# GLA heads of a two-layer streaming encoder: eight places for the running states, the first rows of a head's output fetched early, and a norm's reciprocal root on VectorE

## The chip, the cores and the metric

The kernel runs on one core of a Trainium2 chip. The metric is the device time of one launch in microseconds, as the median of three runs. Traces come from the hardware profiler, of one execution each. TensorE (PE, with its weight loads PEld) multiplies; VectorE (DVE) and ScalarE (ACT) work on what it leaves in PSUM; GpSimd (POOL) and SyncE (SP) mostly issue DMAs, each in the order of its own queue.

## The reference

Two layers, each one pre-normed mixer with a residual, run over 512 frames of a new stream (prompt) and 16 frames of each of 8 running streams (sample), 640 tokens in all. Layer 0 is stick-breaking attention, layer 1 is gated linear attention (GLA) with 4 heads, key width 256 and value width 512. Layer 1 is the part at hand:

```python
b = jnp.cumsum(g, axis=1)
b_last = b[:, -1]
q_in = q * jnp.exp(b)
a = jnp.einsum('bchd,bshd->bhcs', q_in, k * jnp.exp(-b))
a = jnp.where(jnp.tril(jnp.ones((C, C), dtype=bool)), a, 0.0)
o = jnp.einsum('bhcs,bshe->bche', a, v) + jnp.einsum('bchd,bhde->bche', q_in, S)
S = jnp.exp(b_last)[..., None] * S + jnp.einsum('bshd,bshe->bhde', k * jnp.exp(b_last[:, None] - b), v)
...
o = o * lax.rsqrt(jnp.mean(o * o, axis=-1, keepdims=True) + EPS) * g_out.astype(f32).reshape(GLA_HEADS, GLA_DV)
y = (o.reshape(B, T, nv) * jax.nn.silu(r.astype(f32))).astype(h.dtype) @ w_out
```

For the running streams S starts from an input, `state_gla` (8 streams x 4 heads x 256 x 512 floats), and the updated states are an output. Everything is fp32.

## The kernel before, in words

An fp32 product is made of three products of halves in fp32r: every weight block and every row block is split by ScalarE (the high half, L134) and VectorE (the low half, L135, which needs the high one), and TensorE does high x high, low x high and high x low.

The program has one stage after the other; the one at hand is the stage of layer 1's heads. TensorE's order is written out by the program itself: a main line of products (`drive`) is interleaved with side lanes, generators that say by `step` how long they want to wait, counted in a planner's own estimate of TensorE's time. A step may also ask for PSUM banks, and a "tiled" step waits until a planner's interval between tiled groups has passed. This settles in which order instructions are issued; on the chip each engine takes its instructions in the order in which a scheduler has put them, and waits on semaphores. In this stage there are:

- **The main line.** First `others`, 24 parts of the input projection (L653): q and k of heads 1 to 3. Each part is stored to DRAM from a buffer `pl` (two of them). Then `share(0)` and `share(1)` (L699): the first eight of 16 row blocks of the output projection, four column blocks each, with five token blocks added into y. A share's weights come as raw pieces (`wraw`, SyncE's queue) that are then split. After the heads the rest of the output projection (L368), the last column block (L2004) and the final norm follow.
- **The decays** (`decays`): for each head the gates' running sum and its exponentials, applied to q and k (L1638 on TensorE, then ScalarE and VectorE up to k at L1664). Weights `wa2` have two buffers.
- **The prompt lane**: four chunks of 128 tokens for each head. Scores (L1566), masked by `copy_predicated` into one of three tiles `aT` that were zeroed once; products with values and state (L1554); the state's update on VectorE (S, L1757; S1l, L1692). The output is squared and summed by ScalarE (L1579), normed (`rstd_of`, below), scaled by ScalarE (L1583), turned by TensorE (L1601), multiplied with the gate (L1602) and stored as `og` to DRAM from GpSimd's queue.
- **The sample lane**: the 8 running streams. Their states are 64 blocks of 128 x 512 (head, half of the streams e, half of the key dimension dt, pair of streams m), taken in 16 groups of four. For a group TensorE multiplies q with the four states (L1864, eight instructions), then for each state the new k with v (L1870); VectorE updates the state in place (L1872), and GpSimd stores it (L78) and asks for the next state into a free place. There are S0 = 7 places in SBUF, so the n-th state is loaded into the place of state n-7 once that one's store has landed. State numbers in this text count from 0, so group n holds states 4n to 4n+3. The lane asks for its step 13 us of the planner's time after the last request of the group. A norm and an og store as in the prompt lane end a head.
- **The rows** (`fetches`): row blocks of og (128 x 640) come back from DRAM through the `pl` buffers (SyncE), are split into `ogh` and `ogl`, and are what a share multiplies with. For head 0 that begins when the last part has been issued; the first share is then planned once rows 0 to 3 are there.

`rstd_of` makes mean square plus epsilon on VectorE (L232) and takes its power -1/2 on GpSimd (L234), in the same queue as the loads and stores of states, gates and og:

```python
dve.tensor_scalar(ms, ss, 1.0 / n, EPS, op0=ALU.mult, op1=ALU.add)
nc.gpsimd.tensor_tensor(r, ms, mhalf[:, :w], op=ALU.pow)
```

Of the kernel before, what the change touches and what calls it, by code (L numbers as in the profile page):

```python
# [8 lines left out]
F32 = mybir.dt.float32  # L9
F32R = mybir.dt.float32r  # L10
U32 = mybir.dt.uint32
BF16 = mybir.dt.bfloat16
AF = mybir.ActivationFunctionType
ALU = mybir.AluOpType
# [16 lines left out]
ZSCALE = 128 ** -0.5  # L31
TOK = T // P
WR = 2
S0 = 7
GP = 2
NPAIR = HEADS // 2
PLAIN = 2
# [4 lines left out]
def hybrid_step_kernel(ctx: ExitStack, tc: tile.TileContext, A: dict, O: list):  # L42
# [185 lines left out]
    def rstd_of(pool, ss, n, name):  # L228

        w = ss.shape[1]  # L230
        ms = pool.tile([P, w], F32, tag=name + "_ms", name=name + "_ms")
        dve.tensor_scalar(ms, ss, 1.0 / n, EPS, op0=ALU.mult, op1=ALU.add)  # L232
        r = pool.tile([P, w], F32, tag=name + "_r", name=name + "_r")
        nc.gpsimd.tensor_tensor(r, ms, mhalf[:, :w], op=ALU.pow)  # L234
        return r

    def rstd_row(pool, ss, bc, a):

        turned_wide(wide_of(pool, rstd_of(pool, ss, D, "nrm")), bc, a)
# [37 lines left out]
    class Side:  # L277
# [10 lines left out]
        def after(self, wait, what):  # L288

            self.due.append((pe["now"] + wait, what))  # L290
            self.due.sort(key=lambda x: x[0])

        def share(self, **bufs):
            self.free = {k: [0.0] * n for k, n in bufs.items()}
# [387 lines left out]

    y_t = {}

    def share(g, og, w, leave=None, at=None, first=None):


        src = w.rearrange("(kt p) n -> p kt n", p=P)

        def raw(c, i):  # L690
            return wraw(src[:, 4 * g + 2 * i:4 * g + 2 * i + 2, 512 * c:512 * c + 512], 2, 512)

        def products(acc, a, i, w):
            wh, wl = w
            for e in range(2):
                kt = 4 * g + 2 * i + e
                h, lo = (x[:, P * a:P * a + P] for x in og[kt])
# [12 lines left out]
        raws = list(first or [raw(0, 0), raw(0, 1)])  # L710

        def made():
            return [t.rearrange("p (a n) -> p a n", a=2) for t in split(raws.pop(0))]

        w0, w1 = made(), made()
        for c in range(4):
            ws = [w0, w1]
            if c < 3:
                raws += [raw(c + 1, 0), raw(c + 1, 1)]
            if at:  # L720
                at(c)
            each = (0, 1, 2) if leave is add or c < 3 else (4, 1, 2, 3, 0)
            for a in each:
                acc = bank("mm")
                for i in range(2):
                    yield from products(acc, a, i, ws[i])
                leave(a, c, acc)
                if a == each[0] and c < 3:
                    w0 = made()
            if len(each) == 3:  # L730
                acc = {a: bank("mm") for a in (3, 4)}
                for i in range(2):
                    for a in (3, 4):
                        yield from products(acc[a], a, i, ws[i])
                        if i:
                            leave(a, c, acc[a])
                    if i == 0 and c < 3:
                        w1 = made()
# [762 lines left out]
        k0 = 4 * g + 2 * i  # L1501
        return w_out1.rearrange("(kt p) n -> p kt n", p=P)[:, k0:k0 + 2, 512 * c:512 * c + 512]

    with tc.tile_pool(name="gl", bufs=1, reuse_waits="tile") as gl:
        came = {"plain": False, "last": False, "of": 0, "when": 0.0}

        def keep(dst, hh):
            t = []

            def leave(nt, pt):  # L1510
# [11 lines left out]

        others = plain(h2, src, [(n0 + P * hh, keep(dst, hh)) for h in range(1, GH)
                                 for n0, dst in ((256 * h, gq_d[h]), (NK + 256 * h, gk_d[h])) for hh in range(2)],
                       lambda: came.update(plain=True))
        for _ in range(2):
            next(others)

# [24 lines left out]
            for n, (a, b) in enumerate(((0, 0), (0, 1), (1, 0))):  # L1553
                mm(out, l[a], by(l[a], r[b]), start=start and n == 0, stop=stop and n == 2, skip_group_check=True)  # L1554

        masked = [gl.tile([P, P], F32, name=f"aT{n}") for n in range(3)]
        for t in masked:
            nc.gpsimd.memset(t, 0.0)
        turns = {"n": 0}
# [15 lines left out]
        def normed(o):  # L1575

            s1 = gl.tile([P, 1], F32, tag="oss", name="oss", bufs=2)
            on = gl.tile([P, 512], F32, tag="on", name="on", bufs=2)
            act(on, o, AF.Square, accum_out=s1)  # L1579
            return on, rstd_of(gl, s1, 512, "on"), o  # L1580

        def scaled_by(on, r, o):
            act(on, o, AF.Copy, scale=r)  # L1583
# [25 lines left out]
        def decays():  # L1609

            def weights(h):
                wa2 = gl.tile([96, 256], F32R, tag="wa2", name="wa2", bufs=2)
                load(wa2.bitcast(F32), wa2_d[:, 256 * h:256 * h + 256])
                yield step(4.0 if h else 8.0)
                return wa2
# [183 lines left out]
        def sample_lane():  # L1799
# [12 lines left out]
            for h in range(GH):  # L1812
# [43 lines left out]
                for n in range(4):  # L1856
                    dt, e = n // 2, n % 2
                    group = [(h, e, dt, m) for m in range(4)]
                    while any(x not in states for x in group):
                        yield step(0.3)  # L1860
                    yield step(max(since, max(states[x][1] for x in group) + 13.0) - pe["now"], tiled=True)
                    for m in range(4):
                        l = qz[e][:, dt, 32 * m:32 * m + 32]
                        mm(o[32 * m:32 * m + 32, :], l, by(l, states[group[m]][0]), start=False, stop=n == 3,  # L1864
                           skip_group_check=True)
                    for m in range(4):
                        yield step(0.3, tp=1)
                        pt = bank("tp")
                        l = kst[e][:, m, :]
                        mm(pt, l, by(l, vst[:, m, :]), start=True, stop=True)  # L1870
                        s0 = states[group[m]][0]
                        dve.scalar_tensor_tensor(s0, s0, es[:, dt, 2 * m + e:2 * m + e + 1], pt,  # L1872
                                                 op0=ALU.mult, op1=ALU.add)
                        side.after(1.0, lambda x=group[m]: leaves(x))
                    if n == 1:
                        yield from stack(1)
                        yield step(1.5)
# [5 lines left out]
                if h + 1 < GH:  # L1883
                    yield step(4.0)
                    here = fetch(h + 1)

        def fetches():

            def free(kt):
                g, s = kt // 4, kt % 4  # L1890
                return came["plain"] and came["shares"] >= min(2, g if s > 1 else g - 1)

            rows = {}

            def ask_rows(kt):
                rows[kt] = gl.tile([P, T], F32, tag="pl", name="og_in", bufs=2)
                load(rows[kt], og_d[kt // 4][:, kt % 4, :])

            for kt in range(10):
                while min(through.values()) <= kt // 4 or not came["last"]:  # L1900
                    yield step(0.5)
                if kt not in rows:
                    yield step(5.0)
                    ask_rows(kt)
                    if kt % 4 < 3 and kt < 9 and came["plain"]:
                        ask_rows(kt + 1)
                    yield step(4.0)
                while not free(kt):
                    yield step(0.3)
                n = 20 + 2 * kt % 12  # L1910
                og1[kt] = slot(n, name="ogh"), slot(n + 1, name="ogl")
                halves(*og1[kt], rows.pop(kt))
                if kt % 4 < 3 and kt < 9 and kt + 1 not in rows:
                    ask_rows(kt + 1)
                came["rows"], came["at"] = kt + 1, pe["now"]
                yield step(0.5)
# [2 lines left out]
        for x in (decays(), prompt_lane(), sample_lane(), fetches()):  # L1919
            side.add(x)  # L1920
        drive(others)
        with tc.tile_pool(name="w4", bufs=1, reuse_waits="tile") as w4:
            ring3["pool"] = w4
            first = [wraw(w_of(0, 0, i), 2, 512) for i in range(2)]
            for g in range(2):
                side.until(lambda: came["rows"] >= 4 * g + 4 and pe["now"] > came["at"] + 2.0)
                drive(share(g, og1, w_out1, first=first))
                came["shares"] = g + 1
                first = [wraw(w_of(g + 1, 0, i), 2, 512) for i in range(2)]
            ring3["pool"] = None  # L1930
            parts = [split(r) for r in first]
            first = [wraw(w_of(3, 0, i), 2, 512) for i in range(2)]
            side.finish()


    share_banks(mm=8)
# [96 lines left out]
```

## Time and profile before

| | us |
|---|---|
| median of 3 runs (lowest, highest) | 2536.63 (2534.4, 2538.53) |
| the profiled execution | 2535.51 |
| its span | 2533.8 |
| stage of the heads | 1975.4 to 2413.0 |
| TensorE busy over the span | 2429.8 (96%) |
| VectorE, ScalarE, GpSimd busy | 1581.8, 995.2, 163.6 |
| mean granted clock of TensorE | 0.982 |

Rows of the profile read like this: start, duration, engine, line, operation, output<-input by the program's names, shapes, and in brackets the engine's idle time just before with what ended it. A row of waits is "who waits <- for whom: us in total, times, longest". A DMA row on POOL or SP shows its issue; it lands some microseconds later. Lines of the changed program are up to 22 higher than those of the program before (L78 becomes L79, L135 L136, L1864 becomes L1886, L1870 L1892, L699 L716, L653 L670, L1601 L1622).

### The profile page before, as it was taken

How to read it: one execution, taken by the hardware profiler on the slowest of the kernel's cores; microseconds unless marked ns; L12 is line 12 of the kernel's file. 1: busy time of each engine (PE TensorE's matmuls, PEld its weight loads, DVE VectorE, ACT ScalarE, POOL GpSimd, SP SyncE). 2: the span in 40 equal slices, each digit the busy share in tenths (PEclk: the TensorE clock that was granted, in tenths of full speed). 3: DMA queues.
4: the chain of work that ended last, by engine and by line, in shares of the span. 5: the costliest groups of instructions: out<-in, count | busy, mean ns of one | idle time of the engine just before them, and what ended most of it. 6: DMA issues, size and time to landing. Idle time of an engine off the chain costs nothing. (4 is left out here: it accounts for less than half of the span.)

```text
span 2533.8 us, 43960 instructions
## 1 busy us (share of the span) xinstructions
PE 2429.8 (96%) x17561; PEld 2150.1 (85%) x17561; DVE 1581.8 (62%) x2565; ACT 995.2 (39%) x1730; POOL 163.6 (6%) x390
## 2 busy tenths in 40 slices
PE   7899999999999989999999989999999999979998
PEld 5589999999999989888887768999999988857776
DVE  5575555555656655766775678666676565555556
ACT  4342222222223334555442345333333554545223
POOL 0010000000000000000000000000000233342100
PEclk8899999999999999999999999999999999989999
DMA  9966666766654357777864655354434778785634
GB/s 346 327 209 212 223 214 198 241 218 205 219 186 123 113 187 233 260 246 243 267 209 124 214 172 169 96 148 123 125 105 119 212 238 255 217 278 184 228 111 147
DMA packets 469439, 503.13 MB, mean 199 GB/s; under 512 B 42730, under 2 KB 366450, under 8 KB 469106
## 3 DMA queue, kind: packets, MB, share of 16 engines
q1 hardware_dynamic: 446274, 436.60, 54.8%
q0 software_dynamic: 16048, 51.92, 6.1%
q10 hardware_dynamic: 6912, 11.80, 1.3%
q8 instruction: 138, 2.26, 0.4%
q14 instruction: 67, 0.55, 0.1%
HBM read 411.10 MB, written 89.13 MB: 197 GB/s over the span
## 5 line engine op out<-in xcount | busy, mean ns | idle before, releaser
L594 PE MATMUL ps_mm<-sums,wh 128*128 128x320 f32 x2752 | 613.7, 311 | 1.5 <-ACT wh L134 1.5
L594 PE MATMUL ps_mm<-h,wh 128*128 128x320 f32 x2064 | 461.8, 312 | 5.7 <-DVE u L600 4.6
L594 PEld LDWEIGHTS ps_mm<-sums,wh 128*128 128x128 f32 x2752 | 458.3, 188 | 10.4 <-issue 7.4
L594 PE MATMUL ps_mm<-sums,wl 128*128 128x320 f32 x1376 | 425.8, 309 | 0.7 <-DVE wl L135 0.7
L135 DVE TENSOR_TENSOR wl<-wr,wh 128x1024 fp32r<-128x1024 f32 x193 | 236.1, 1224 | 244.0 <-ACT wh L134 243.2
L594 PEld LDWEIGHTS ps_mm<-h,wh 128*128 128x128 f32 x2064 | 343.2, 188 | 21.8 <-issue 13.0
L134 ACT CAST wh<-wb 128x1024 fp32r<-128x1024 f32 x170 | 178.4, 1049 | 426.1 <-PE ps_mm L594 352.8
L134 ACT CAST wh<-wr 128x1024 fp32r<-128x1024 f32 x193 | 202.6, 1050 | 346.6 <-PE ps_mm L594 184.6
L594 PE MATMUL ps_mm<-h,wl 128*128 128x320 f32 x1032 | 319.2, 309 | 0.0
L653 PE MATMUL ps_mm<-h,wh 128*128 128x320 f32 x1152 | 265.2, 318 | 5.3 <-ACT pl L1514 3.1
L594 PEld LDWEIGHTS ps_mm<-sums,wl 128*128 128x128 f32 x1376 | 258.4, 188 | 1.0 <-DVE wl L135 1.0
L135 DVE TENSOR_TENSOR wl<-wb,wh 128x1024 fp32r<-128x1024 f32 x170 | 207.9, 1223 | 60.5 <-ACT wh L134 60.1
L653 PEld LDWEIGHTS ps_mm<-h,wh 128*128 128x128 f32 x1152 | 193.0, 189 | 21.7 <-issue 11.4
L699 PE MATMUL ps_mm<-wh,ogh 128*128 128x512 f32 x450 | 197.4, 439 | 4.2 <-DVE y L704 2.7
L594 PEld LDWEIGHTS ps_mm<-h,wl 128*128 128x128 f32 x1032 | 193.8, 188 | 0.0
L653 PE MATMUL ps_mm<-h,wl 128*128 128x320 f32 x576 | 178.5, 310 | 0.0
L699 PE MATMUL ps_mm<-wh,ogl 128*128 128x512 f32 x450 | 177.9, 395 | 0.3 <-DVE ogl L135 0.3
L699 PE MATMUL ps_mm<-wl,ogh 128*128 128x512 f32 x450 | 177.7, 395 | 0.0
L699 PEld LDWEIGHTS ps_mm<-wh,ogh 128*128 128x128 f32 x450 | 85.6, 190 | 29.6 <-issue 14.4
L653 PEld LDWEIGHTS ps_mm<-h,wl 128*128 128x128 f32 x576 | 108.8, 189 | 0.0
L699 PEld LDWEIGHTS ps_mm<-wh,ogl 128*128 128x128 f32 x450 | 85.0, 189 | 20.3 <-DVE ogl L135 0.7
L518 PE MATMUL ps_mm<-wh,h 128*128 128x512 f32 x252 | 93.4, 432 | 5.9 <-ACT h L134 2.8
(355 smaller groups left out, 3747.0 us busy)
## 6 DMA issues: line engine op xcount, KB each, us to landing
ar<-in_w_ada_dram SPq DMA_DIRECT2D x160, 512.0 KB
wb<-in_sb_w_in_dram SPq DMA_DIRECT2D x82, 512.0 KB
kc<-in_cache_sb_k_dram SPq DMA_DIRECT2D x64, 512.0 KB
vc<-in_cache_sb_v_dram SPq DMA_DIRECT2D x64, 512.0 KB
wr<-in_gla_w_in_dram SPq DMA_DIRECT2D x51, 512.0 KB
wb<-in_gla_w_in_dram SPq DMA_DIRECT2D x45, 512.0 KB
wr<-in_sb_w_in_dram SPq DMA_DIRECT2D x44, 512.0 KB
ar<-in_w_ada_dram SPq DMA_DIRECT2D x64, 256.0 KB
```

Of the source, the lines that this page charges most:

```text
L134: nc.scalar.copy(hi, x)
L135: (e or dve).tensor_tensor(lo, x, hi.bitcast(F32), op=ALU.subtract)
L518: mm(acc[a], l, by(l, r[:, e, :]), start=j == 0 and e == 0 and begun, stop=j == 7 and e == 1 and last)
L594: mm(acc, l[:, k, :], by(l[:, k, :], r), start=start and k == 0 and first, stop=k == 7 and last, skip_group_check=True)
L653: mm(acc[nt], l[:, k, :], by(l[:, k, :], r), start=k0 == 8 and k == 0 and first, stop=k0 == 0 and k == 7 and last)
L699: mm(acc, l, by(l, r[:, e, :]), start=i == 0 and e == 0 and first, stop=i == 1 and e == 1 and last)
```

## The change

Four things are changed in the stage of the heads, and nothing ahead of it:

1. S0 is 8 instead of 7. The space for it comes from one `wa2` buffer less, and from two of the masked tiles, which are put into adaLN tables that are no longer read (`sh_t[1]`, `sc_t[1]`).
2. `rstd_dve` replaces `rstd_of` for the 20 norms of the heads: an integer guess of the reciprocal root, a cubic and a quadratic Newton step, nine VectorE instructions on 128x1, none on GpSimd. The norms of the layers and the final one keep `rstd_of`.
3. Rows 0 to 2 of head 0's output are loaded early into two tiles that the shares' split weights use later (row 2 in two pieces, so there is one load and one split more), and are split when the last but one part has ended. Row 3 and all later ones come through `pl` as before. The first share is begun inside the last part: its two first weight pieces are loaded and the first is split there.
4. The sample lane asks for an ordinary step at 9 us of the planner's time after the request, then for a tiled one, instead of a tiled one at 13 us. Some waits between looks are 0.3 instead of 0.5.

```diff
-S0 = 7
+S0 = 8
...
+    def rstd_dve(pool, ss, n, name):
+
+        ms, r, t, u = (pool.tile([P, 1], F32, tag=f"{name}_{x}", name=f"{name}_{x}", bufs=2 if x == "r" else 1) for x in ("ms", "r", "t", "u"))
+        dve.tensor_scalar(ms, ss, 1.0 / n, EPS, op0=ALU.mult, op1=ALU.add)
+        dve.tensor_scalar(r.bitcast(I32), ms.bitcast(I32), -0.5, float(0x5F3759DF), op0=ALU.mult, op1=ALU.add)
+        for cubic in (True, False):
+            dve.scalar_tensor_tensor(t, r, ms, r, op0=ALU.mult, op1=ALU.mult)
+            if cubic:
+                dve.tensor_scalar(u, t, 0.375, -1.25, op0=ALU.mult, op1=ALU.add)
+                dve.tensor_scalar(u, t, u, 1.875, op0=ALU.mult, op1=ALU.add)
+            else:
+                dve.tensor_scalar(u, t, -0.5, 1.5, op0=ALU.mult, op1=ALU.add)
+            dve.tensor_tensor(r, r, u, op=ALU.mult)
+        return r
...
-        w0, w1 = made(), made()
+        w0 = made()
+        if apart:
+            yield
+        w1 = made()
...
-                       lambda: came.update(plain=True))
+                       lambda: upper())
...
-        masked = [gl.tile([P, P], F32, name=f"aT{n}") for n in range(3)]
+        masked = [t[1].rearrange("p k r -> p (k r)")[:, :P] for t in (sh_t, sc_t)] + [gl.tile([P, P], F32, name="aT2")]
...
-            return on, rstd_of(gl, s1, 512, "on"), o
+            return on, rstd_dve(gl, s1, 512, "on"), o
...
-                wa2 = gl.tile([96, 256], F32R, tag="wa2", name="wa2", bufs=2)
+                wa2 = gl.tile([96, 256], F32R, tag="wa2", name="wa2")
...
-                    yield step(max(since, max(states[x][1] for x in group) + 13.0) - pe["now"], tiled=True)
+                    yield step(max(since, max(states[x][1] for x in group) + 9.0) - pe["now"])
+                    yield step(0.0, tiled=True)
...
+        def upper():
+            came.update(plain=True)
+            begun.append(share(0, og1, w_out1, first=[wraw(w_of(0, 0, i), 2, 512) for i in range(2)], apart=True))
+            next(begun[0])
...
+            x = [w4.tile([P, 1024], F32, tag=t, name="og_in") for t in ("wh", "wl")]
+            for n in range(2):
+                load(x[n][:, :T], og_d[0][:, n, :])
+            load(x[0][:, T:], og_d[0][:, 2, :1024 - T])
+            load(x[1][:, T:2 * T - 384], og_d[0][:, 2, 1024 - T:])
+            while not came["plain"]:
+                yield step(0.3)
+            for kt in range(2):
+                halves(*row(kt), x[kt][:, :T])
+                yield step(0.8)
+            to = row(2)
+            halves(*[t[:, :1024 - T] for t in to], x[0][:, T:])
+            halves(*[t[:, 1024 - T:] for t in to], x[1][:, T:2 * T - 384])
...
-            for kt in range(10):
+            for kt in range(3, 10):
...
-                drive(share(g, og1, w_out1, first=first))
+            drive(share(g, og1, w_out1, first=first) if g else begun[0])
```

GpSimd's queue around the load of state 47, the last of group 11, before. `s_23211` is state 40, whose place state 47 (`s_23486`) takes:

```order
L234 TENSOR_TENSOR on_r<-on_ms,mhalf 128x1
L78 DMA og_93<-gate 512x1x128
L78 DMA out_dram<-S 128x2x512
L78 DMA out_dram<-s_23211 128x512
L78 DMA out_dram<-s_23225 128x512
L78 DMA out_dram<-s_23227 128x512
L78 DMA gate<-gr_106 128x4x128
L78 DMA out_dram<-s_23339 128x512
L78 DMA og_93<-gate 512x1x128
L78 DMA s_23486<-in_state_gla_dram 128x512
```

The same with the change. State 47 is `s_23519`; it takes the place of state 39 (`s_22815`), and state 40 is `s_23329`:

```order
L79 DMA out_dram<-s_22773 128x512
L79 DMA out_dram<-s_22784 128x512
L79 DMA out_dram<-s_22803 128x512
L79 DMA s_23491<-in_state_gla_dram 128x512
L79 DMA out_dram<-s_22815 128x512
L79 DMA s_23493<-in_state_gla_dram 128x512
L79 DMA s_23511<-in_state_gla_dram 128x512
L79 DMA og_93<-gate 512x1x128
L79 DMA s_23519<-in_state_gla_dram 128x512
L79 DMA gate<-gr_105 128x4x128
L79 DMA og_93<-gate 512x1x128
L79 DMA out_dram<-s_23329 128x512
```

The load of state 47 has moved ahead of the store of state 40, the first of the group before it, and the root is gone from the queue.

TensorE's order at the end of the parts (`others`), before: the last two rows of L653, then the sample lane, a norm's transposes and head 3's decay, the states of group 11 (L1864), and the first share's products (L699):

```order
L653 MATMUL ps_mm<-h,wh 128x320 x2
L653 MATMUL ps_mm<-h,wl 128x320
L1870 MATMUL ps_tp<-vst,kst_20578 128x512 x3
L1601 MATMUL ps_tp<-ident,on 128x128 x4
L1638 MATMUL ps_tp<-alr_in,wa_22802 128x320 x2
L1864 MATMUL ps_z<-s_23356,qz_20577 32x512
L1864 MATMUL ps_z<-s_23378,qz_20577 32x512
L1864 MATMUL ps_z<-s_23402,qz_20577 32x512
L1864 MATMUL ps_z<-s_23486,qz_20577 32x512
L1870 MATMUL ps_tp<-vst,kst_20579 128x512
L699 MATMUL ps_mm<-wh,ogh 128x512
```

The same place with the change:

```order
L670 MATMUL ps_mm<-h,wh 128x320 x2
L670 MATMUL ps_mm<-h,wl 128x320
L1622 MATMUL ps_tp<-ident,on 128x128 x4
L1886 MATMUL ps_z<-s_23329,qz_20579 32x512
L1886 MATMUL ps_z<-s_23347,qz_20579 32x512
L1886 MATMUL ps_z<-s_23359,qz_20579 32x512
L1886 MATMUL ps_z<-s_23385,qz_20579 32x512
L1575 MATMUL ps_tp<-v,krh 128x512 x2
L1575 MATMUL ps_tp<-v,krl 128x512
L1892 MATMUL ps_tp<-vst,kst_20581 128x512 x4
L716 MATMUL ps_mm<-wh,ogh 128x512
```

The group at the border is now group 10 (states 40 to 43), not 11, whose products come inside the share.

VectorE's order at the same place, before: a norm's only VectorE step among the state updates and the splits of og rows:

```order
L135 TENSOR_TENSOR ogl<-og_in,ogh 128x640
L1838 TENSOR_TENSOR kc<-kd,kc 128x4x32
L1872 SCALAR_TENSOR_TENSOR s_23356<-s_23356,es,ps_tp 128x512
L232 TENSOR_SCALAR on_ms<-oss 128x1
L1872 SCALAR_TENSOR_TENSOR s_23378<-s_23378,es,ps_tp 128x512
L1872 SCALAR_TENSOR_TENSOR s_23402<-s_23402,es,ps_tp 128x512
L135 TENSOR_TENSOR ogl<-og_in,ogh 128x640
L1872 SCALAR_TENSOR_TENSOR s_23486<-s_23486,es,ps_tp 128x512
```

With the change, from the updates of group 10 to the end of that norm (the row in it is row 4; row 3 stands some rows ahead):

```order
L1894 SCALAR_TENSOR_TENSOR s_23329<-s_23329,es,ps_tp 128x512
L1894 SCALAR_TENSOR_TENSOR s_23347<-s_23347,es,ps_tp 128x512
L246 TENSOR_SCALAR on_u<-on_t 128x1
L1894 SCALAR_TENSOR_TENSOR s_23359<-s_23359,es,ps_tp 128x512
L1778 SCALAR_TENSOR_TENSOR S<-S,el,ps_tp 128x512
L1894 SCALAR_TENSOR_TENSOR s_23385<-s_23385,es,ps_tp 128x512
L247 TENSOR_SCALAR on_u<-on_t,on_u 128x1
L136 TENSOR_TENSOR ogl<-og_in,ogh 128x640
L250 TENSOR_TENSOR on_r<-on_r,on_u 128x1
L244 SCALAR_TENSOR_TENSOR on_t<-on_r,on_ms 128x1
L249 TENSOR_SCALAR on_u<-on_t 128x1
L250 TENSOR_TENSOR on_r<-on_r,on_u 128x1
```

The norm's steps now stand between the updates, and a row's split stands between its steps.

More of the change, by code (lines that the diff above doesn't have):

```diff
@@ L11 @@
 U32 = mybir.dt.uint32
+I32 = mybir.dt.int32
 BF16 = mybir.dt.bfloat16
@@ L290, in after @@
             self.due.append((pe["now"] + wait, what))
+            self.due.sort(key=lambda x: x[0])
             self.due.sort(key=lambda x: x[0])
@@ L683, in hybrid_step_kernel, with share @@
     y_t = {}
-    def share(g, og, w, leave=None, at=None, first=None):
+    def share(g, og, w, leave=None, at=None, first=None, apart=False):
         src = w.rearrange("(kt p) n -> p kt n", p=P)
@@ L1502, in w_of @@
         return w_out1.rearrange("(kt p) n -> p kt n", p=P)[:, k0:k0 + 2, 512 * c:512 * c + 512]
-    with tc.tile_pool(name="gl", bufs=1, reuse_waits="tile") as gl:
+    with tc.tile_pool(name="gl", bufs=1, reuse_waits="tile") as gl, \
+            tc.tile_pool(name="w4", bufs=1, reuse_waits="tile") as w4:
         came = {"plain": False, "last": False, "of": 0, "when": 0.0}
@@ L1885, in sample_lane, with row @@
                     here = fetch(h + 1)
+        begun = []
+        def upper():
+            came.update(plain=True)
+            begun.append(share(0, og1, w_out1, first=[wraw(w_of(0, 0, i), 2, 512) for i in range(2)], apart=True))
+            next(begun[0])
+        def row(kt):
+            n = 20 + 2 * kt % 12
+            og1[kt] = slot(n, name="ogh"), slot(n + 1, name="ogl")
+            return og1[kt]
         def fetches():
@@ L1890, in free @@
                 g, s = kt // 4, kt % 4
-                return came["plain"] and came["shares"] >= min(2, g if s > 1 else g - 1)
+                return came["shares"] >= min(2, g if s > 1 else g - 1)
+            while min(through.values()) < 1:
+                yield step(0.5)
+            yield step(8.0)
+            x = [w4.tile([P, 1024], F32, tag=t, name="og_in") for t in ("wh", "wl")]
[11 more added lines that the diff above has]
+            halves(*[t[:, 1024 - T:] for t in to], x[1][:, T:2 * T - 384])
+            came["rows"], came["at"] = 3, pe["now"]
             rows = {}
@@ L1897, in ask_rows @@
                 load(rows[kt], og_d[kt // 4][:, kt % 4, :])
-            for kt in range(10):
+            for kt in range(3, 10):
                 while min(through.values()) <= kt // 4 or not came["last"]:
-                    yield step(0.5)
+                    yield step(0.3)
                 if kt not in rows:
-                    yield step(5.0)
+                    if kt > 3:
+                        yield step(5.0)
                     ask_rows(kt)
-                    if kt % 4 < 3 and kt < 9 and came["plain"]:
+                    if 3 < kt < 9 and kt % 4 < 3:
                         ask_rows(kt + 1)
@@ L1909, in fetches @@
                     yield step(0.3)
-                n = 20 + 2 * kt % 12
-                og1[kt] = slot(n, name="ogh"), slot(n + 1, name="ogl")
-                halves(*og1[kt], rows.pop(kt))
+                halves(*row(kt), rows.pop(kt))
                 if kt % 4 < 3 and kt < 9 and kt + 1 not in rows:
@@ L1921, in hybrid_step_kernel @@
         drive(others)
-        with tc.tile_pool(name="w4", bufs=1, reuse_waits="tile") as w4:
+        for g in range(2):
+            side.until(lambda: came["rows"] >= 4 * g + 4 and pe["now"] > came["at"] + 2.0)
             ring3["pool"] = w4
-            first = [wraw(w_of(0, 0, i), 2, 512) for i in range(2)]
-            for g in range(2):
-                side.until(lambda: came["rows"] >= 4 * g + 4 and pe["now"] > came["at"] + 2.0)
-                drive(share(g, og1, w_out1, first=first))
[L1928 to L1933, printed above, removed]
+            drive(share(g, og1, w_out1, first=first) if g else begun[0])
+            came["shares"] = g + 1
+            first = [wraw(w_of(g + 1, 0, i), 2, 512) for i in range(2)]
+        ring3["pool"] = None
+        parts = [split(r) for r in first]
+        first = [wraw(w_of(3, 0, i), 2, 512) for i in range(2)]
+        side.finish()
     share_banks(mm=8)
```

## The prediction

> **What bounds the kernel now.** I read the page first. Its rows give the span, TensorE's busy time, and below them TensorE's busy tenths in 40 slices.
>
> ```profile
> span 2533.8 us, 43960 instructions
> PE 2429.8 (96%) x17561; PEld 2150.1 (85%) x17561; DVE 1581.8 (62%) x2565; ACT 995.2 (39%) x1730; POOL 163.6 (6%) x390
> PE   7899999999999989999999989999999999979998
> ```
>
> TensorE is the bound: 96% busy, and from the third slice on only one falls to 7, the 36th (2217 to 2280 us). This is where layer 1's heads end. The whole stage of the heads runs from 1975.4 to 2413.0 us. What TensorE waited for from 1960 us on, and one such row of ScalarE (total, times, longest):
>
> ```profile
> PE ps_z L1864 <- DMA s<-in_state_gla_dram: 23.4, 3, 17.4
> PE ps_tp L1566 <- DVE k L1664: 1.6, 1, 1.6
> PE ps_tp L1554 <- ACT on L1583: 0.4, 1, 0.4
> ACT on L1583 <- POOL on_r L234: 16.8, 11, 3.7
> ```
>
> So 23.4 us are three waits for a GLA state of the sample streams to land, and nothing else is near. TensorE's timeline has them one by one, and the table of windows has what the two long ones leave behind (busy us of PE, PEld, DVE, ACT, POOL, then PEclk, DMA share, GB/s):
>
> ```profile
> 2081.52 1.04 PE L1864 MATMUL ps_z<-s,qz 128*32 128x512 f32 x2 [0.26 <-DMA s<-in_state_gla_dram]
> 2170.20 1.92 PE L1864 MATMUL ps_z<-s,qz 128*32 128x512 f32 x2 [5.69 <-DMA s<-in_state_gla_dram]
> 2264.32 1.92 PE L1864 MATMUL ps_z<-s,qz 128*32 128x512 f32 x2 [17.44 <-DMA s<-in_state_gla_dram]
> ...
> 1975.40:2413.00 437.60, 404.93 (x2292) 344.49 (x2293) 247.49 (x421) 213.77 (x390) 126.78 (x218) 0.97 0.73 230
> 2080.00:2120.00 40.00, 38.10 (x246) 34.71 (x245) 22.50 (x45) 21.30 (x43) 15.69 (x28) 1.00 0.81 254
> 2164.50:2170.20 5.70, 0.01 (x2) 0.00 (x0) 3.06 (x8) 1.98 (x6) 3.31 (x6) 0.79 0.85 295
> 2170.20:2174.70 4.50, 4.50 (x11) 2.74 (x12) 0.86 (x4) 1.67 (x4) 0.71 (x2) 0.50 0.36 113
> 2246.90:2264.30 17.40, 0.00 (x0) 0.00 (x0) 10.57 (x18) 7.86 (x14) 5.25 (x9) 0.58 0.93 322
> 2264.30:2270.20 5.90, 5.88 (x12) 3.36 (x13) 1.56 (x3) 1.58 (x4) 2.20 (x4) 0.50 0.58 207
> ```
>
> After the 5.69 us the granted clock is 0.50 for 4.5 us, after the 17.44 us for 5.9 us: half of that work is lost too, 2.25 + 2.95 = 5.2 us. The wait of 1.6 us for k, which lies in 2080 to 2120, left the clock at 1.00. What can be won by state waits is thus 23.4 + 5.2 = 28.6 us.
>
> [...]
>
> Why the states come late. State n is loaded into the place of state n-7, so after that state's last use (its product L1870, then the update L1872) and its store. TensorE's rows of three such L1870, and two rows beside the last for the pitch; then GpSimd's queue:
>
> ```profile
> 2068.65 0.39 PE L1870 MATMUL ps_tp<-vst,kst 128*128 128x512 f32 x1
> 2153.25 0.48 PE L1870 MATMUL ps_tp<-vst,kst 128*128 128x512 f32 x1
> 2241.99 0.39 PE L1870 MATMUL ps_tp<-vst,kst 128*128 128x512 f32 x1
> 2242.22 0.46 PE L653 MATMUL ps_mm<-h,wh 128*128 128x320 f32 x2
> 2242.51 0.31 PE L653 MATMUL ps_mm<-h,wl 128*128 128x320 f32 x1
> ...
> 2077.97 0.55 POOL L78 DMA_DIRECT2D s<-in_state_gla_dram  x1 [2.52 <-DMA out_dram<-s]
> 2161.30 0.72 POOL L78 DMA_DIRECT2D og<-gate  x1 [6.08 <-DVE y L1640]
> 2166.77 1.77 POOL L78 DMA_DIRECT2D s<-in_state_gla_dram  x3
> 2245.28 0.59 POOL L78 DMA_DIRECT2D out_dram<-s  x1
> 2258.89 0.72 POOL L78 DMA_DIRECT2D og<-gate  x1 [5.99 <-DVE ogl L135]
> 2259.53 1.68 POOL L78 DMA_DIRECT2D s<-in_state_gla_dram  x3
> ```
>
> From L1870 to the use of the refilled place it took 2081.52 - 2068.65 = 12.9 us, 2170.20 - 2153.25 = 16.9 and 2264.32 - 2241.99 = 22.3. In the two long ones the load stood in GpSimd's queue behind an og store that idled 6.08 and 5.99 us. TensorE had only 4.9 us of other work between the last pair (22.33 - 17.44), and 11.3 between the second.
>
> **The change part by part.** *Eight places.* A group has four states, so with eight every state refills a place whose group was finished a whole group earlier. I counted TensorE's work between each such L1870 and the use of its place in the new order, at the pitches of the rows above (0.23 us for 512 columns, 0.145 for 320): the least is 19.1 us, the others 19.6 to 57. Against chains of 12.9 to 22.3 us this leaves 0 to 3.2 us of state waits; I take 0.5, since only the longest chain at the least distance gives 3.2. The half clock goes with them, as long as no new wait is as long as 5.69.
>
> *Early rows 0 to 2, and the first share begun in the last part.* In the old order the state wait also covered this (SyncE's issue of the og rows, then VectorE's second half of their split; the last row is ScalarE's scaling of a norm):
>
> ```profile
> 2250.15 0.32 SPq L71 DMA_DIRECT2D og_in<-og  x1
> 2251.86 10.46 SPq L71 DMA_DIRECT2D og_in<-og  x3
> 2257.67 0.83 DVE L135 TENSOR_TENSOR ogl<-og_in,ogh 128x640 fp32r<-128x640 f32 x1 [1.08 <-ACT ogh L134]
> 2261.14 0.83 DVE L135 TENSOR_TENSOR ogl<-og_in,ogh 128x640 fp32r<-128x640 f32 x1 [0.70 <-ACT ogh L134]
> L1583 ACT ACTIVATE on<-ps_tp,on_r x16: 681/688/696, 2027.7 to 2338.8; 128x512 f32<-128x512 f32 x16
> ```
>
> Rows 2 and 3 were split at 2258.5 and 2261.97, so without the early rows the share could not have begun before 2262 and some 15 of the 17.44 us would have stayed. A row takes 8.4 to 10.1 us from issue to the end of its split (2250.15 to 2258.50, 2251.86 to 2261.97). Row 3 still comes that way: TensorE has 14.0 us from the matmul that frees its load to its first use, so it costs nothing, but it now covers nothing: row 4's load waits for row 3's split (same buffer), and row 4's split stands in VectorE's queue inside a norm, ahead of its last four steps. That norm's transposes (L1622) come 16.9 us of TensorE after row 3's load is freed; two rows one behind the other take 16.7 to 20.2, the norm's four steps (0.19 each, below) and the scaling of 0.69 another 1.4. Late by 1.2 to 4.7, unless the transfers are quicker at a DMA share below the 0.93 of that window; 0 to 5, I take 2. Behind that split on VectorE stand the next norm, a gate product and state updates, which GpSimd's stores wait for; their places are not needed for 19 us.
>
> *Norms.* 20 norms lose a step on GpSimd and gain eight on VectorE:
>
> ```profile
> L232 DVE TENSOR_SCALAR on_ms<-oss x20: 128/148/154, 2026.8 to 2353.1; 128x1 f32<-128x1 f32 x20
> L234 POOL TENSOR_TENSOR on_r<-on_ms,mhalf x20: 559/567/672, 2027.1 to 2353.3; 128x1 f32<-128x1 f32 x20
> L1106 DVE TENSOR_SCALAR w<-w,later x32: 265/273/275, 953.9 to 1346.5; 128x1 f32<-128x1 f32 x32
> 2526.87 0.16 DVE L1971 TENSOR_REDUCE ssf<-ss4f 128x1 f32<-128x4 f32 x1 [0.85 <-ACT junk L1966]
> 2527.06 0.15 DVE L232 TENSOR_SCALAR fin_ms<-ssf 128x1 f32<-128x1 f32 x1
> ```
>
> The old way takes 2027.1 - 2026.8 + 0.57 = 0.87 us. Nine dependent steps take 9 x 0.19 = 1.7 us by the two last rows, 9 x 0.27 = 2.5 at most by L1106. So each norm is 0.8 to 1.6 us later, 16 to 32 us over all twenty if TensorE waited for each, and nothing if its other work covers them. The old rows are nearer to nothing: ScalarE waited 16.8 us for GpSimd's root, and TensorE 0.4 for ScalarE's result. GpSimd's queue loses 20 x 0.57 = 11 us and the stops ahead of them. VectorE gains 160 x 0.15 to 0.27 = 24 to 43 us on its 247.5 of 437.6. I take 1.5 us.
>
> [...]
>
> *The rest.* The sample lane asks for its state step 9 us (the planner's) after the request, not 13: this only sets the order. One decay buffer less, and two masks in old tables, cost nothing, since the weights of a head's decay are read a head ahead. Decays may move against their use: the old 1.6 us may come back as 0 to 3, I take 0.5 more.
>
> **Sum.** 28.6 - 0.5 - 2 - 1.5 - 0.5 = 24.1 us. The profiled execution took 2535.51 us, so 2511.4; the runs' median is 1.1 above it: 2512.5. All bounds at their best give 2508, or 2505 with the 1.6 and the smaller gaps gone too; at their worst (3.2 + 5 + 3 for the norms + 3 = 14, fully exposed norms being a rival), 2535.5 - 28.6 + 14 = 2521.
>
> **Rivals.** *The wait moves to the pair's border (0.16).* Rows 3 and 4, the norm and the share's second weight piece meet on VectorE, whose 10.57 us in the 17.4 us window show how much it does there while TensorE stands. If TensorE stops there as long as 5.69 us, the clock halves again: 5 to 10 + 2.9 us, so some 2519 to 2528. Against it: rows 0 to 2 are split well before.
>
> *VectorE's norms hold TensorE (0.08), the slower side.* In VectorE's order other work stands between the steps of a norm, so one can take far longer than 2.5 us. It becomes slower than before from (28.6 + 5)/20 = 1.7 us for each of twenty norms; at 2 us the time is 2535.5 - 28.6 + 40 = 2547. Against it: 0.4 us of such waits so far, and two thirds of VectorE's time at most in the new stage ((247.5 + 43)/413 = 70%).
>
> *Nothing comes of it (0.07).* If transfers bounded the heads, all freed time would come back as a wait for weights and the time stay at 2534 to 2537. Against it: 230 GB/s over the stage would rise to 230 x 437.6/413.5 = 243, and 322 was reached in one window.
>
> **How the numbers follow.** The forecast has 0.69, with its own range 2505 to 2519. The range 2504 to 2528 takes in the first rival and leaves out the two others and some ends, under 2 in 10. A measurement of this kernel can tell 0.2%, 5 us, from no change: forecast and first rival are faster (0.85), the third is the same (0.07), the second slower (0.08).
>
> **What would show it.** TensorE's waits for s<-in_state_gla_dram below 3.2 us in all; no window at clock 0.50 inside the heads; the 36th slice at 9; og rows 0 to 2 split before the last part ends; the largest wait in the heads under 5 us and at L1622 near the first L716. Wrong would be: a wait of over 5 us at the first L716 or L1622, TensorE waiting for on (L1604) more than 5 us in all, or a longer stretch after the heads than the old 2533.8 - 2413.0 = 120.8 us.

## The result and the profile after

The changed kernel takes 2518.9 us (median of 6 runs, 2515.42 to 2523.97) against 2535.86 for the kernel before (6 runs, 2533.37 to 2540.05): a ratio of 0.9931, 95% interval 0.9916 to 0.9947. That is 17 us faster; 24.1 had been forecast. The profiled execution took 2523.97 us, 5 above its median. Its stage of the heads starts 5.5 us later than in the profile of before (1980.84 against 1975.36), after work that is the same in both programs, so stages are compared here, not ends.

The page after (span, busy time, TensorE's busy tenths in 40 slices), what TensorE waited for from 1960 us on, and its two longest waits as rows of the timeline:

```profile
span 2522.3 us, 44090 instructions
PE 2431.6 (96%) x17561; PEld 2154.8 (85%) x17561; DVE 1601.9 (64%) x2726; ACT 994.4 (39%) x1731; POOL 151.2 (6%) x370
PE   7899999999999999999999989999999999999998
...
PE ps_tp L1622 <- ACT on L1604: 6.9, 3, 5.5
PE ps_mm L716 <- ACT y L724: 3.4, 2, 3.0
PE ps_mm L670 <- ACT pl L1535: 2.5, 1, 2.5
PE ps_tp L1892 <- DVE s L1894: 1.3, 1, 1.3
...
2257.57 0.50 PE L716 MATMUL ps_mm<-wh,ogh 128*128 128x512 f32 x1 [2.97 <-ACT y L724]
2336.59 1.12 PE L1622 MATMUL ps_tp<-ident,on 128*128 128x128 f32 x4 [5.49 <-ACT on L1604]
```

The waits for states, 23.4 us before, are gone without a rest, and the 36th slice is at 9 (the parts end there; the heads, which the prediction names, run on to 2413.0). In their place stand waits that were hardly there: 6.9 us for a norm's scaled output, 3.4 us for ScalarE to clear a PSUM bank of the share.

The stage and its clock in the table of windows (busy us of PE, PEld, DVE, ACT, POOL, then PEclk, DMA share, GB/s):

```profile
1980.80:2401.20 420.40, 402.40 (x2292) 345.21 (x2292) 267.45 (x582) 212.19 (x391) 114.22 (x198) 0.98 0.75 240
2009.90:2012.40 2.50, 0.05 (x1) 0.05 (x1) 2.39 (x5) 2.42 (x6) 0.00 (x0) 1.00 0.18 45
2012.80:2016.20 3.40, 3.40 (x15) 3.40 (x14) 2.03 (x5) 3.37 (x5) 0.00 (x0) 0.50 0.43 122
2258.50:2261.90 3.40, 3.40 (x10) 2.62 (x9) 2.52 (x6) 2.76 (x8) 2.31 (x5) 0.50 0.82 292
2333.60:2340.40 6.80, 3.81 (x11) 3.23 (x12) 4.02 (x8) 1.08 (x2) 2.28 (x4) 0.50 0.62 212
```

The stage takes 420.4 us instead of 437.6. TensorE's idle time in it fell from 437.6 - 404.9 = 32.7 to 18.0 us, by 14.7; its busy time by 2.5. The clock is still halved three times, with 3.40 + 3.40 + 3.81 us of work in it, 5.3 us lost; before it was 5.2. After the heads 121.1 us remain, as before (120.8).

The first of the three halved stretches (2012.80 to 2016.20) stands ahead of the first norm of the heads (2033) and of all rows. It follows the 2.5 us wait for `pl`, whose copy on ScalarE (2011.89) stands behind the split of a weight piece that had not landed:

```profile
2008.55 1.05 ACT L135 CAST wh<-wr 128x1024 fp32r<-128x1024 f32 x1 [3.13 <-DMA wr<-in_gla_w_in_dram]
```

The kernel before waits 1.6 us at this place, with no halved clock after it (1.00 from 2006.00 to 2009.40). In the profiles of the experiments the halved stretch there comes and goes: norms on VectorE alone, in the order of before, have it (after a wait of 3.4 us), and the changed kernel with rows 8 and 9 gated does not (0.6 us). So these 1.7 us of half clock can't be put down to the change.

Where the two waits come from. First VectorE inside the norm for which TensorE waits 5.49 us, then ScalarE and SyncE's load of the rows concerned (8 and 9 of og):

```profile
2324.71 0.15 DVE L241 TENSOR_SCALAR on_ms<-oss 128x1 f32<-128x1 f32 x1 [1.00 <-ACT on L1600]
...
2331.48 0.83 DVE L136 TENSOR_TENSOR ogl<-og_in,ogh 128x640 fp32r<-128x640 f32 x1 [1.06 <-ACT ogh L135]
2332.22 0.21 DVE L244 SCALAR_TENSOR_TENSOR on_t<-on_r,on_ms 128x1 f32<-128x1 f32 x1
...
2334.81 0.15 DVE L249 TENSOR_SCALAR on_u<-on_t 128x1 f32<-128x1 f32 x1
2334.87 0.82 DVE L136 TENSOR_TENSOR ogl<-og_in,ogh 128x640 fp32r<-128x640 f32 x1
2335.60 0.15 DVE L250 TENSOR_TENSOR on_r<-on_r,on_u 128x1 f32<-128x1 f32 x1
...
2330.73 0.72 ACT L135 CAST ogh<-og_in 128x640 fp32r<-128x640 f32 x1 [2.02 <-DMA og_in<-og]
2335.85 0.69 ACT L1604 ACTIVATE on<-ps_tp,on_r 128x512 f32<-128x512 f32 x1 [1.86 <-DVE on_r L250]
...
2326.70 1.97 SPq L72 DMA_DIRECT2D og_in<-og  x2
```

From the first to the last step of this norm 11 us pass. Its own nine steps are 0.15 to 0.22 us each; the rest is work put between them, above all two splits of rows that were asked for at 2326.70 and had not landed.

ScalarE before the 2.97 us wait:

```profile
2254.27 0.73 ACT L135 CAST ogh<-og_in 128x640 fp32r<-128x640 f32 x1 [2.59 <-DMA og_in<-og]
2255.01 1.28 ACT L1664 ACT_TABLE_LOAD   x1
2256.95 0.57 ACT L724 COPY y<-ps_mm 128x512 f32<-128x512 f32 x1
```

The copy that frees the share's PSUM bank stands behind the split of row 5, for which ScalarE idles 2.59 us, and behind a table load of 1.28 us.

### The profile page after: what moved, and what is told of

Its sections match the earlier page's. It is cut to its first block, busy times and chain, and to the rows that moved or that the text cites. A ratio compares the mean times of both kernels' runs of the same rounds, so it can differ in the third digit from the quotient of the medians.

```text
span 2522.3 us, 44090 instructions
## 1 busy us (share of the span) xinstructions
PE 2431.6 (96%) x17561; PEld 2154.8 (85%) x17561; DVE 1601.9 (64%) x2726; ACT 994.4 (39%) x1731; POOL 151.2 (6%) x370
## 4 chain that ended last, share of the span: by engine, by line
PE 77%; DMA 7%; DVE 5%; ACT 3%; issue 2%; SPq 0%; POOL 0%; ACTq 0%; POOLq 0%; DVEq 0%
PE ps_mm L611 38%; PE ps_mm L716 10%; PE ps_mm L670 7%; PE ps_mm L385 3%; DMA gv<-kr 2%; PE ps_tp L1102 2%; PE ps_tp L1575 2%; PE ps_mm L535 1%; PE ps_tp L1154 1%; PE ps_tp L1062 1%; PE ps_z L1038 1%; DMA og_in<-og 1%; PE ps_z L181 1%; PE ps_mm L2053 1%; PE ps_z L1116 1%
```

## The experiments

The working theory was: what was lost of the forecast is og rows whose splits stand in the in-order queues of ScalarE and VectorE before their row has landed. The rivals: VectorE's 160 extra steps slow it everywhere, or a part of the change is not worth what the forecast took it for. Every time here is the median of a run's executions with the kernel before on the same chip beside it (2536.3 to 2539.9 us). Ratios are also compared across the three chips used, which takes a kernel's ratio to be the same on each; only the change itself was measured twice (0.9931 and 0.9927). Where an expectation gives microseconds, 1 us is about 0.0004. The pieces of the change are taken apart at the end of the section, in a table.

**Root back on GpSimd.** One line of the changed kernel; TensorE's order stays the same, instruction for instruction.

```diff
-            return on, rstd_dve(gl, s1, 512, "on"), o
+            return on, rstd_of(gl, s1, 512, "on"), o
```

> The changed kernel, but the 20 norms of the heads take their root on GpSimd again; TensorE's order is the same, instruction for instruction. Theory (splits of og rows stand in VectorE's and ScalarE's queues before their row has landed, and hold what is behind them): the 5.5 us wait at L1622 (2331 in the changed kernel) lies inside a VectorE norm whose last steps stand behind two such splits; with the root on GpSimd it goes, with its 1.9 us of half clock, while the 3.0 us wait for y before the second share column stays: about 2512 (2509 to 2515). Rival A (VectorE's 160 extra steps slow the heads everywhere): all new waits go, 2507 or less. Rival B (the root in GpSimd's queue was what made states late): states late again, 2521 or more.

Measured: 2519.44 us, 0.9918 (0.9900 to 0.9936). The 5.5 us wait at L1622 went as the theory has it (1.4 us in all are left there), and the wait for y stayed (2.7 us). The forecast of about 2512 us was missed: the ratio can't be told from the change's 0.9931. The profile has new waits behind the root on GpSimd, one of 3.8 us for k and one of 2.2 us for `pl`. Both rivals are out: the new waits did not go as a whole, and no state was late.

**Gated splits.** The splits of rows 4, 5, 8 and 9 may start only after a given number of y blocks has left PSUM, through a small copy into the split's target. Loads, norms and TensorE's order are those of the changed kernel.

```diff
+            held, first_y = {4: 3, 5: 6, 8: 24, 9: 26}, [len(made_y)]
...
-                halves(*row(kt), rows.pop(kt))
+                to = row(kt)
+                if kt in held:
+                    while len(made_y) < first_y[0] + held[kt]:
+                        yield step(0.3)
+                    nc.scalar.copy(to[0][:, :2], made_y[-1][:, :2])
+                halves(*to, rows.pop(kt))
```

> The changed kernel, but the splits of rows 4, 5, 8 and 9 may only start after a certain column block of y has been left (a 128x2 copy on ScalarE in front of each split); loads and TensorE's order unchanged, norms on VectorE. Theory: no split stands before its row has landed, so the 5.5 us wait at L1622 and the 3.0 us wait for y go with their 1.9 + 1.7 us of half clock: 2519 - 12 = about 2507 (2505 to 2511). Rival A (VectorE's extra steps): little changes, 2516 to 2521.

Measured: 2508.23 us, 0.9878 (0.9860 to 0.9895), below the change and apart from its interval. The waits of TensorE in the stage, the stage in the windows, and the last steps of the same norm on VectorE:

```profile
PE ps_tp L1624 <- ACT on L1606: 3.0, 3, 1.5
PE ps_mm L717 <- ACT y L725: 2.2, 2, 1.2
...
1972.40:2383.20 410.80, 398.64 (x2292) 342.76 (x2293) 267.02 (x582) 212.40 (x395) 114.20 (x198) 1.00 0.76 245
...
2318.52 0.15 DVE L250 TENSOR_TENSOR on_r<-on_r,on_u 128x1 f32<-128x1 f32 x1
2318.71 0.22 DVE L244 SCALAR_TENSOR_TENSOR on_t<-on_r,on_ms 128x1 f32<-128x1 f32 x1
2318.96 0.15 DVE L249 TENSOR_SCALAR on_u<-on_t 128x1 f32<-128x1 f32 x1
...
2319.82 0.15 DVE L250 TENSOR_TENSOR on_r<-on_r,on_u 128x1 f32<-128x1 f32 x1
```

No wait over 1.5 us is left at the two places, the stage takes 410.8 us, and the norm's last four steps take 1.5 us together. VectorE has as much to do as in the change (267.0 against 267.5 us), so its load is not what held TensorE. For the wait at L1622 the theory holds. For the wait for y it is not shown: a second profile of the changed kernel (below) has 1.1 us at most there without any gate, while the wait at L1622 is 5.4 us again.

**Rows 8 and 9 gated alone.** The same with `{8: 24, 9: 26}`.

> The changed kernel with the splits of rows 8 and 9 alone gated. Theory: the 5.5 us wait at L1622 in the second half goes (to about 1.5) with its 1.9 us of half clock, the 3.0 us wait for y in the first share stays: ratio 0.990 to 0.992, between the change (0.993) and both gates (0.988). Rival (one of the two gates does it all): 0.988 or 0.993.

Measured: 2511.51 us, 0.9889 (0.9874 to 0.9904). The wait at L1622 in the second half fell to 1.5 us. The ratio is a little better than expected; in this profile the wait for y was 1.4 us at most although rows 4 and 5 are free, so gating them may add little. The intervals of both gates overlap.

**Gated splits with the root on GpSimd.**

> The changed kernel with the gated splits of rows 4, 5, 8 and 9 and with the root on GpSimd. Theory: with the splits gated nothing holds a VectorE norm any more, while a root on GpSimd still stands behind state transfers: slower than gated with VectorE norms (0.988), 0.990 to 0.993. Rival (VectorE's extra steps cost several us that the gate hid): 0.987 or less.

Measured: 2520.86 us, 0.9926 (0.9913 to 0.9940), as the theory has it. ScalarE's wait for GpSimd's root, and TensorE's two largest:

```profile
ACT on L1606 <- POOL on_r L235: 25.0, 11, 6.9
...
PE ps_mm L670 <- ACT pl L1537: 6.4, 2, 3.2
PE ps_tp L1589 <- DVE k L1687: 5.1, 2, 3.8
```

The root stands in GpSimd's queue behind state transfers, ScalarE behind the root, and behind ScalarE the longest wait for k (3.8) and one of the two for `pl` (3.1); the other one (3.2) is the early one, ahead of the norms. So the norms on VectorE are worth 0.5% of the time (0.9878 against 0.9926) once the splits are gated, and nothing measurable without it (0.9931 and 0.9918).

**Norms on VectorE alone**, in the kernel before; TensorE's order is that of before.

> The kernel before with the 20 norms of the heads on VectorE and nothing else; TensorE's order is that of before. Theory: stores of states are free of the root in GpSimd's queue, but a place still comes free too late; norms are covered: state waits stay at 15 to 25 us, 2531 to 2540. Rival A: clearly slower, above 2545. Rival B (root in GpSimd's queue made states late): the two long state waits shrink, below 2528.

Measured: 2540.66 us, 1.0004 (0.9995 to 1.0014). Neither rival's time came; the theory's did, as a ratio, but not its waits. TensorE's waits for norms and states, and below them the last use of a place (L1886), a wait for a norm and the use of the state that refills the place:

```profile
PE ps_tp L1617 <- ACT on L1599: 12.5, 3, 7.5
PE ps_z L1880 <- DMA s<-in_state_gla_dram: 11.2, 2, 5.9
...
2244.25 0.39 PE L1886 MATMUL ps_tp<-vst,kst 128*128 128x512 f32 x1
2254.27 1.12 PE L1617 MATMUL ps_tp<-ident,on 128*128 128x128 f32 x4 [7.54 <-ACT on L1599]
2263.05 1.91 PE L1880 MATMUL ps_z<-s,qz 128*32 128x512 f32 x2 [5.27 <-DMA s<-in_state_gla_dram]
```

The waits for states are half as long as before (11.2 against 23.4 us), but that is not what a queue without the root gave. The wait of 5.69 us is still there (5.94). The one of 17.44 is down to 5.27, and 8.8 us ahead of it TensorE now waits 7.54 us for a norm, whose steps on VectorE stand behind the split of a row. From the last use of the place to the use of the new state 18.8 us pass (2244.25 to 2263.05), 22.3 before: the state comes 3.5 us sooner, and for the rest it is TensorE that comes later.

**Eight places alone**, with the masks in the old tables and one decay buffer less, in the kernel before.

> The kernel before with eight places only (masks in the old tables, one decay buffer less); GpSimd's roots, rows and the lane's 13 us as before. Theory: state waits go to 0 to 3 us, but the first share still waits for rows 2 and 3 at the end of the parts: 5.7 + 2.2 us won, and only a few of the 17.4: 2521 to 2530. Rival (the state wait was all there was at the border): 2507 to 2512.

Measured: 2542.99 us, 1.0012 (1.0002 to 1.0023). This is the clearest miss: all state waits are gone and nothing is gained. TensorE's waits; then the longest of them, with the norm's step on VectorE and GpSimd's queue:

```profile
PE ps_tp L1601 <- ACT on L1583: 27.3, 4, 12.8
...
2263.55 0.69 PE L1601 MATMUL ps_tp<-ident,on 128*128 128x128 f32 x2 [12.83 <-ACT on L1583]
2248.06 0.15 DVE L232 TENSOR_SCALAR on_ms<-oss 128x1 f32<-128x1 f32 x1
2260.84 0.56 POOL L78 DMA_DIRECT2D s<-in_state_gla_dram  x1 [1.14 <-DMA og<-gate]
2261.97 0.71 POOL L234 TENSOR_TENSOR on_r<-on_ms,mhalf 128x1 f32<-128x1 f32 x1
```

VectorE has the mean square at 2248.06, and the root comes at 2261.97: it stands behind two loads and two stores of states, an og store and six loads of values in GpSimd's queue. In the place of the waits for states (23.4 us) stand waits for norms (27.3). Not all of that is the root's: ScalarE comes to this norm's scaling at 2262.82 from a cast for the sample lane (2262.61) that it had itself waited for, so both ended at nearly the same time. The next run differs from this one by the root alone and shows its share.

**Eight places and norms on VectorE**, without early rows and with the old ask.

> The kernel before with eight places and the norms on VectorE; rows and the lane's 13 us as before. TensorE's order is that of the run with eight places alone. Each of the two alone gave nothing (ratios 1.001 and 1.000). Theory (each takes away the wait that the other leaves: with the places the states, with the root off GpSimd's queue the norms): together they win, but without early rows the norms and the first share at the end of the parts still wait for splits of rows 0 to 3: ratio 0.995 to 0.999. Rival (the early rows add nothing): 0.993, as the whole change. Rival (no interaction): 1.001.

Measured: 2529.61 us, 0.9965 (0.9952 to 0.9978), as expected. The places take the waits for states, and the norms on VectorE take about half of the waits for norms, from 27.3 to 13.2 us (8.4 of them at the end of the parts); 5.7 us are for the share's y.

**The changed kernel with seven places.**

> The changed kernel with seven places instead of eight, all else as changed (TensorE's order follows the planner, so some states are asked for later). Theory: the states are late again, 10 to 25 us of waits for them: ratio 0.998 to 1.004. Rival (a GpSimd queue without roots is fast enough for seven): 0.992 to 0.995.

Measured: 2549.52 us, 1.0034 (1.0022 to 1.0045). The waits for states return only in part (9.2 us), but the planner asks later, and the sample lane now ends behind the second share, with 10.2 us of waits for its own keys. The eighth place is needed in the changed order.

**The old ask** in the changed kernel, **no early rows** in the changed kernel (eight places, norms on VectorE, new ask), and the changed kernel once more, on one chip:

> The changed kernel with the sample lane's old ask (one tiled step 13 us of the planner's after the request). Theory: with eight places a state has landed before either step, so the ask only moves the order: ratio 0.991 to 0.995, as the change. Rival (the earlier ask is part of the gain): 0.996 or more.

> The kernel before with eight places, VectorE norms and the lane's new ask, but without the early rows and the early share. Theory: what lies between eight places with VectorE norms (0.9965) and the change (0.993) is the early rows, so this stays at 0.995 to 0.998, with a wait of some 8 us at L1617 or the first share at the end of the parts. Rival (it was the ask): 0.993.

> The changed kernel once more, on the chip of the two others: 0.9916 to 0.9947 again.

Measured: old ask 2522.10 us, 0.9942 (0.9929 to 0.9954); no early rows 2518.49 us, 0.9928 (0.9917 to 0.9940); the change 2519.24 us, 0.9927 (0.9914 to 0.9939). The old ask is as expected; its profile has 15.4 us of waits for norms. The expectation for the second was wrong: the early rows add nothing to the change as it is. TensorE's waits without early rows, then in the change on the same chip:

```profile
PE ps_tp L1617 <- ACT on L1599: 5.2, 4, 3.1
PE ps_mm L715 <- ACT ogh L135: 2.9, 2, 2.1
...
PE ps_tp L1622 <- ACT on L1604: 7.3, 4, 5.4
```

Without early rows TensorE waits at the end of the parts (3.1 for a norm, 2.9 for row splits), but 1.4 us at most in the second half; the change has the 5.4 us wait there again. My new theory was that the early rows win at the border what that wait gives back.

**No early rows, gated.** This tests it: the same gate in the kernel without early rows.

> The kernel before with eight places, VectorE norms, the new ask and the gated splits of rows 4, 5, 8 and 9, but without the early rows and the early share; TensorE's order is that of the same kernel ungated (0.9928). Theory (the early rows are worth what the border of the parts costs without them, some 6 us of waits and their half clock, and in the change this was given back by the 5.4 us wait at L1622): here there is no such wait to gate, so 0.990 to 0.993 against 0.988 with early rows. Rival (early rows are worth nothing): 0.988.

Measured: 2516.07 us, 0.9905 (0.9889 to 0.9922), where the theory puts it, against 0.9878 (0.9860 to 0.9895) with early rows. The intervals just overlap, so that early rows are worth something with the gate is likely, not settled.

The pieces together (ratio to the kernel before):

| places | root | ask | early rows | gate | ratio |
|---|---|---|---|---|---|
| 8 | GpSimd | 13 | no | no | 1.0012 |
| 7 | VectorE | 13 | no | no | 1.0004 |
| 8 | VectorE | 13 | no | no | 0.9965 |
| 8 | VectorE | 13 | yes | no | 0.9942 |
| 8 | VectorE | 9 | no | no | 0.9928 |
| 8 | VectorE | 9 | yes | no | 0.9931, 0.9927 (the change) |
| 7 | VectorE | 9 | yes | no | 1.0034 |
| 8 | GpSimd | 9 | yes | no | 0.9918 |
| 8 | GpSimd | 9 | yes | yes | 0.9926 |
| 8 | VectorE | 9 | yes | rows 8, 9 | 0.9889 |
| 8 | VectorE | 9 | no | yes | 0.9905 |
| 8 | VectorE | 9 | yes | yes | 0.9878 |

The last is the fastest and beats both kernels; from the one with rows 8 and 9 alone gated it can't be told apart.

## Why the prediction was right, and where it was not

*State waits.* Right: forecast 0.5 us, measured none. The count of TensorE's work between a place's last use and its next held.

*The half clock.* This step failed. I took 5.2 us as won, "as long as no new wait is as long as 5.69". Waits of 2.5 and 2.97 us were each followed by 3.4 us at 0.50, and the one of 5.49 by a halved stretch of 6.8. So the half clock's loss stayed at 5.3 us; 1.7 us of it, behind the 2.5 us wait, can't be put down to the change (see above). The two gated kernels with early rows and norms on VectorE have no halved clock after the first 40 us of the stage; the one with all four gates has a mean of 1.00 over its stage.

*New waits.* I had 4.5 us; TensorE's idle time outside the state waits grew from 9.3 to 18.0 us, by 8.7. The mechanism was named: a row's split inside a norm's steps, its row not yet landed. But I priced it at row 4 only, and there TensorE lost nothing. The scaling of that norm ended at 2247.13, and its transposes began at 2247.18, straight behind products of the share, since TensorE had itself come later: by 1.28 us for the norm before it and by 1.32 us for a state's update. In the former ScalarE's queue was held by the share's second weight piece rather than by a row:

```profile
2235.12 1.05 ACT L135 CAST wh<-wr 128x1024 fp32r<-128x1024 f32 x1 [2.23 <-DMA wr<-in_gla_w_out_dram]
2236.07 0.68 ACT L1604 ACTIVATE on<-ps_tp,on_r 128x512 f32<-128x512 f32 x1
...
2236.81 0.66 PE L1622 MATMUL ps_tp<-ident,on 128*128 128x128 f32 x4 [1.28 <-ACT on L1604]
2247.18 0.66 PE L1622 MATMUL ps_tp<-ident,on 128*128 128x128 f32 x4
```

The 5.49 us came at rows 8 and 9, between the two shares, which I had not looked at. The 2.97 us at the second column of the share, ScalarE's copy behind row 5, I had not seen at all; it is the first rival's place with another instruction, and 2518.9 us lies at the very end of the forecast's own range (2505 to 2519), where that rival's times (2519 to 2528) begin. The runs spread over 8.6 us, so that the median fell on the forecast's side is luck. Two of the signs that I had named as wrong came: over 5 us at an L1622, and over 5 us in all for `on`. Idle short by 8.7 - 4.5 = 4.2 us and busy time by 5.2 - 2.5 = 2.7 make the 6.9 between 24.1 and the stage's 17.2. Of the busy time, 2.5 us fell although the half clock cost the same. They come from the products with the states, before and after:

```profile
L1864 PE MATMUL ps_z<-s,qz 128*32 128x512 f32 x128 | 21.9, 619 | 23.4 <-DMA s<-in_state_gla_dram 23.4
L1886 PE MATMUL ps_z<-s,qz 128*32 128x512 f32 x128 | 17.0, 605 | 0.0
```

A whole group of eight takes 1.07 us, and where a wait breaks the group, its last two products take another 1.04 to 1.92 us by the prediction's three rows. That is 4.9 us before and none after, while the shares' products and the norms' transposes took 2.2 us more.

*Eight places as the whole gain.* The sum was near, its reason was not. I put all 28.6 us to the places and called the move of the norms a cost, reading the old 0.4 us as its worth. Alone the places gave nothing (1.0012): the norms then came as late as the states had, about half of it by the root in GpSimd's queue, as the run with both shows. That queue loses 11 us, I wrote, and gave it no price. The failed step is to count on a wait in a profile where another one, behind it at the same place, ends almost as late (TensorE went on at 2264.32 before and at 2263.55 with the places alone).

*Early rows.* I had put some 15 of the 17.44 us on them. In the kernel with the new ask they change nothing measurable (0.9928 and 0.9927), and I had called the ask one that "only sets the order": eight places and VectorE norms go from 0.9965 to 0.9928 by the ask alone, which is 9 us that the sum has at nothing. What early rows are worth shows at most with the old ask (0.9965 to 0.9942, 6 us) and in the gated pair (0.9905 to 0.9878, 7 us); in both the intervals just overlap. That the terms were wrong in both directions and the sum still came near is luck too.

*Norms on VectorE, the slower side.* Not so: their steps are 0.15 to 0.22 us, 1.6 us together, and with the gate they win. A single norm did take 11 us, by what stood between its steps.

*Nothing comes of it.* Not so: the stage moved its bytes at 240 GB/s instead of 230, the gated one at 245.

*Small slips of the sum.* The worst case, 2521 us, leaves out the 1.1 us between the profiled execution and the median that the best case, 2508, has; and 70% is a little more than two thirds. Neither moves the forecast.

## What to carry to other kernels

A wait read from a profile is worth no more than its distance to the next one that ends at the same place: before counting on it, ask which instruction behind it would have been late anyway, and in whose queue. Work that waits for a DMA (a split of a loaded block) should not stand in an in-order engine ahead of the small steps that TensorE needs next; here a cheap dependence on a later result (four small copies, with ScalarE busy for 212.4 us of the stage against 212.2) kept the scheduler from putting it there, and a wait of 5.5 us fell to 1.5. Take several parts of such a change apart and together, since two of them can each be worth nothing alone (1.0012 and 1.0004) and something together (0.9965).

## What the runs showed of the hardware

The halved clock came in stretches of 3.4 us (twice) and 6.8 us in the changed kernel, and of 6.8 and 20.4 us in the kernel before. Behind the waits of 5.49, 5.69 and 17.44 us it began inside the wait, 2.5, 3.3 and 2.9 us after its start; behind those of 2.5 and 2.97 us it began 0.4 and 0.9 us after TensorE had gone on. Of the kernel before, in the table of windows:

```profile
2167.80:2174.60 6.80, 4.40 (x11) 2.64 (x12) 1.59 (x5) 2.02 (x5) 1.70 (x4) 0.50 0.55 184
2249.80:2270.20 20.40, 5.88 (x12) 3.36 (x13) 9.23 (x17) 7.73 (x16) 6.60 (x12) 0.50 0.82 275
```

These are the 4.5 and 5.9 us of the prediction, seen from where they start. A wait's length alone does not settle whether half clock follows: it followed the wait of 2.5 us (the row 2009.90 to 2012.40 above), while in the run with the old ask a wait of 3.04 us at the same place was followed by full clock, 1.00 in the 1.40 us of the row:

```profile
2004.60 0.56 PE L670 MATMUL ps_mm<-h,wh 128*128 128x320 f32 x2 [3.04 <-ACT pl L1535]
2004.60:2006.00 1.40, 1.40 (x9) 1.40 (x10) 0.67 (x3) 1.39 (x2) 0.00 (x0) 1.00 0.97 242
```
